# One input projection for two chunks: eight block products become seven, and the attention of those chunks is issued beside the third

## The chip, the cores and the metric

The kernel runs on one core of one Trainium2 chip. The metric is the device time of one execution, the median of the runs. Everything is float32. The engines are named as in the profile: PE (matmul), PEld (the loading of PE's weights), DVE (vector), ACT (scalar), POOL and SP, whose queue issues all DMAs here.

## The reference, cut to what matters

One encoder layer is applied to 1280 tokens: 1024 of a prompt and 256 of a sample, model width 1024.

```
h = x + 0.5 * swiglu(rmsnorm(x), gate, up, down)          # D_FF 2816
u = rmsnorm(h); proj = u @ w_in                           # 1024 -> 2816
aq, ak, av, rq, rk, rv, rg = split(proj)                  # 512,128,128,512,512,512,512
attn = rmsnorm(windowed attention with sink logits(rotate(aq), rotate(ak), av))
ret  = silu(rg) * norm(retention forward + retention backward(rotate(rq), rotate(rk), rv))
h = h + concat(attn, ret) @ w_out
h = h + 0.5 * swiglu(rmsnorm(h), gate2, up2, down2); y = rmsnorm(h)
```

The attention looks 128 tokens to both sides. Prompt and sample do not see each other.

## The kernel before, in words

**Layout.** Tokens lie along the free dimension, features along the 128 partitions. There are three chunks (`CH`, line 21): 0 and 1 are the two halves of the prompt, 512 tokens each, chunk 2 is the sample, 256 tokens. A "unit" is 128 output columns of a weight matrix with all 1024 rows; `w_in` has 22 units: four of `aq` (`UQ`), one each of `ak` (`UK`) and `av` (`UV`), four each of `rq`, `rk`, `rv` and of the gates `rg` (`URQ`, `URK`, `URV`, `URG`, line 23).

**Exactness.** Every operand of a large product is split into a high and a low fp32r half (`split`, line 510: one ACT copy, one DVE subtraction), and `part` (line 528) issues three matmuls for each 128 rows: high by high, high by low, low by high. One unit for one chunk is thus 8 x 3 = 24 matmuls.

**Stages.** The first feed-forward layer (`ffn`, line 655) already multiplies chunks 0 and 1 together by a seven-product scheme: `combos` (line 611) forms four sums of the activation blocks, `seven` (line 621) four sums of the weight blocks, and `product` (line 664) accumulates the seven products. `down_last` (line 793) ends the layer chunk by chunk. Then `project` (line 1044) computes each unit for each chunk: 22 units for chunk 0, 22 for chunk 1, 22 for chunk 2, and each time the unit's weights are fetched and split again. The result is rotated with tables (DVE), transposed on PE (the values), or put through Silu (the gates), and stays in SBUF; only the gates of chunk 0 go out to DRAM. The attention (`attention`, line 1081, eight blocks of 128 queries) and the retention (`retention`, line 1150, four heads) of chunks 0 and 1 are issued between the twelve head units of chunk 1; chunk 2's 22 projections come after them, with `cat_split(0)` (line 1239: norm and split of chunk 0's results) among them. `out_unit` (line 1249) is the product with `w_out`; then comes the second feed-forward layer.

**What sets the order.** `Weaver` (line 100) records all operations and plans their order: `arrange` (line 268) simulates the five engines with a cost for each operation (line 142) and takes, for each engine, the earliest operation of the program that is ready; operations of other engines than PE have priorities from the time at which PE needs them (`due`, line 254). The planned order of each engine is then fixed. An SP operation may be planned at most `AHEAD = 300` recorded operations before PE's front. Nearly all SBUF tiles are of one tag, `s2`: 104 buffers of 128x512 float32, and `may` (line 306) refuses an operation for which no buffer would be free. PSUM has eight banks under one tag. All calls go through line 438, so every row of the trace carries this line, and groups are told apart by the tiles' names: `pa` is a bank of the projections and feed-forward products, `pb` a bank of `down`, transposes and others, `pc` one of the scores; `wh` and `wl` are the halves of weights, `xh`, `xl` or `x` those of activations (`x` where W is 256).

Of the kernel before, what the change touches and what calls it, by code (L numbers as in the profile page):

```python
# [12 lines left out]
P = 128  # L13
# [86 lines left out]
class Weaver:  # L100
# [4 lines left out]
    MARGIN = 0.4  # L105
    AHEAD = 300
    PASSES = 4
    ENG = {"tensor": "PE", "vector": "DVE", "scalar": "ACT", "gpsimd": "POOL", "sync": "SP"}

    def __init__(self, tc):  # L110
# [157 lines left out]
    def arrange(self, prio):  # L268
# [37 lines left out]
        def may(op):  # L306
            if op.eng == "SP" and op.idx > front() + self.AHEAD:
                return False
            op.allocs = fresh(op)
            for b in op.allocs:  # L310
                t = self.tags[b.tag]
                need = sum(x.tag == b.tag for x in op.allocs)
                if len(t["free"]) < need:
                    return False
                gt = sorted(t["live"], reverse=True)
                j = 0
                m = b.order - 1
# [31 lines left out]
        table = None  # L349
        out = []  # L350
        SLACK = 0.15
        while len(out) < len(ops):
            best = None
            for e in engs:
                lim = free[e] + SLACK
                while later[e] and later[e][0][0] <= lim:
                    i = heapq.heappop(later[e])[1]
                    heapq.heappush(now[e], (prio[i], i))
                held = []
                pick = None  # L360
# [12 lines left out]
                if pick is None:  # L373
                    for r, i in sorted(later[e])[:40]:
                        if may(ops[i]):
                            pick = (r, i)
                            break
                if pick is not None:
                    op = ops[pick[1]]
                    start = pick[0]  # L380
                    for b in op.allocs:
                        start = max(start, min(self.tags[b.tag]["free"]))
                    if best is None or start < best[0]:
                        best = (start, pick[1], e)
            start, i, e = best
            op = ops[i]
            if (prio[i], i) in now[e]:
# [63 lines left out]
def tile_encoder_layer(ctx: ExitStack, tc: tile.TileContext, xT, wf1, w_in, w_out, wf2,  # L451
# [166 lines left out]
        nc.vector.scalar_tensor_tensor(t4, n2, -1.0, b21, op0=ALU.mult, op1=ALU.subtract)  # L618
        return {i: pair(t, 512) for i, t in ((6, n2), (7, t3), (5, t1), (4, t4))}

    def seven(r11, r12, r21, r22, W, together=False):

        if W > 256:
            s1, s2_, s3, s4 = (s2(name=n) for n in ("s1", "s2", "s3", "s4"))
# [12 lines left out]
        yield 21, halves(r21, W, together)  # L637
        nc.vector.tensor_tensor(s4, s2_, r12, op=ALU.add)
        yield 3, halves(s4, W, together)

# [275 lines left out]
    us = {}  # L916
    spill = {}

    def finish1(c):
        us[c] = norm_split(h[c], G_MIX, CH[c][1])  # L920

    def load1(c, d):
        return load_x(c, d, d + 1)[0]
# [63 lines left out]
    ffn(1, wf1, lead1(), lambda a: factors((a.n[0], a.n[1]), (a.pairs[0], a.pairs[1])), load1, after1, 1)  # L987


    mask = s2(name="mask")  # L990
    nc.sync.dma_start(mask[:, :384], cmat[:, 128:512])
    nc.sync.dma_start(cols, cmat[:, 512:520])
    sink8 = nc.tile(cpool, [P, 8], F32, None, "sink8", 1)
    nc.vector.tensor_scalar(sink8, par[:, SINK:SINK + 8], 8.0, None, op0=ALU.mult)
    dec = {}
    for name, ld, col in (("wf", LDF, 0), ("wb", LDB, 1), ("cf", LDF, 4), ("cb", LDB, 4)):
        t = nc.tile(cpool, [P, 4], F32, None, name, 1)
        nc.vector.tensor_scalar(t, par[:, ld:ld + 4], cols[:, col:col + 1], None, op0=ALU.mult)
        nc.scalar.activation(t, t, AF.Exp)
        if name[0] == "w":  # L1000
            nc.vector.tensor_scalar(t, t, KSC, None, op0=ALU.mult)
        dec[name] = t
    Dm = s2(name="Dm").rearrange("p (h i) -> p h i", h=4)
    rowf = s2(name="rowf").rearrange("p (h i) -> p h i", h=4)
    rowb = s2(name="rowb").rearrange("p (h i) -> p h i", h=4)
    ctm = s2(name="ctm")
    nc.sync.dma_start(ctm, cmat[:, 520:1032])
    ctr = s2(name="ctr")
    nc.sync.dma_start(ctr[:, 0:256], cmat[:, 1032:1288])
    for hh in range(4):  # L1010
        lf, lb = par[:, LDF + hh:LDF + hh + 1], par[:, LDB + hh:LDB + hh + 1]
        t1 = big(256, name="dt")
        nc.scalar.activation(t1[:, 0:128], ctm[:, 0:128], AF.Exp, scale=lf)
        nc.scalar.activation(t1[:, 128:256], ctm[:, 256:384], AF.Exp, scale=lb)
        nc.vector.tensor_tensor(t1[:, 0:128], t1[:, 0:128], ctm[:, 128:256], op=ALU.mult)
        nc.vector.tensor_tensor(t1[:, 128:256], t1[:, 128:256], ctm[:, 384:512], op=ALU.mult)
        nc.vector.tensor_tensor(t1[:, 0:128], t1[:, 0:128], t1[:, 128:256], op=ALU.add)
        nc.vector.tensor_scalar(Dm[:, hh, :], t1[:, 0:128], KSC, None, op0=ALU.mult)
        nc.scalar.activation(rowf[:, hh, :], ctr[:, 0:128], AF.Exp, scale=lf)
        nc.scalar.activation(rowb[:, hh, :], ctr[:, 128:256], AF.Exp, scale=lb)  # L1020


    o = {}

    pairs = {}
# [8 lines left out]
    def tables(c):  # L1034
        c0, W = CH[c]
        p0 = c0 if c < 2 else 0
        tabs = []
        for i in range(4):
            t = s2(name="tab")
            nc.sync.dma_start(t[:, :W], rope[:, i, p0:p0 + W])  # L1040
            tabs.append(t)
        return tabs

    def project(c, u, tabs):
        c0, W = CH[c]
        nb = W // P
        cosa, sina, cosr, sinr = tabs
        w = unit(w_in[u])
        ps = bank_a()
        lin(ps, w, us[c], W)  # L1050
        ps = ps[:, :W]
        out = new_out(c, u)[:, :W]
        o[c, u] = out
        if u >= URG:
            nc.scalar.activation(out, ps, AF.Silu)
            if c == 0:
                d = nc.tile(dp, [P, 512], F32, None, f"rg_{u}", 1)
                nc.sync.dma_start(d, out)
                o[c, u] = d
            return  # L1060
        t = big(W, name="rt")[:, :W]
        if u == UV or u >= URV:
            nc.scalar.copy(t, ps)
# [4 lines left out]
            return  # L1068
        if u <= UK:
            cos, sin = cosa, sina  # L1070
            nc.vector.stream_shuffle(t, ps, mask=SWAP)
        else:
            cos, sin = cosr, sinr
            nc.scalar.copy(t[0:64], ps[64:128])
            nc.scalar.copy(t[64:128], ps[0:64])
        nc.vector.tensor_tensor(out, ps, cos[:, :W], op=ALU.mult)
        nc.vector.tensor_tensor(t, t, sin[:, :W], op=ALU.mult)
        nc.vector.tensor_tensor(out, out, t, op=ALU.add)


    def attention(c, blk, chunks):
# [68 lines left out]
    def retention(hh, chunks):  # L1150
# [33 lines left out]
        for c in chunks:  # L1184
# [48 lines left out]
            if c == 0:  # L1233
# [26 lines left out]
            h[c][d] = t  # L1260


    lead = [UK, UV] + list(range(UQ, UQ + 4))
    heads = [b + hh for hh in range(4) for b in (URK, URV, URQ)]
    gates = list(range(URG, URG + 4))
    pr = (0, 1)
    tabs = tables(0)
    for i, u in enumerate(gates + [UV] + list(range(URV, URV + 4)) + [UK, 0, 1, 2, 3] + list(range(URQ, URV))):
        project(0, u, tabs)
        if i == 2:  # L1270
            finish1(1)
        if i == 5:
            finish1(2)
    tabs = tables(1)
    for u in gates + lead:
        project(1, u, tabs)
    todo = [(0, b) for b in range(4)] + [(1, b) for b in range(4)]
    for i, u in enumerate(heads):
        project(1, u, tabs)
        if i % 3 != 0:  # L1280
            attention(*todo.pop(0), pr)
        if i % 3 == 2:
            retention(i // 3, pr)
    tabs = tables(2)
    cat = {}
    for i, u in enumerate(gates + lead + heads):
        if i == 14:
            cat[0] = cat_split(0)
        project(2, u, tabs)
    for d in range(KT):  # L1290
        out_unit(0, d, cat[0])
        if d < 4:
# [131 lines left out]
```

## Time and profile before

| | |
|---|---|
| median of 3 runs | 2288.32 us (2284.65 to 2289.14) |
| the profiled execution, its own time | 2286.97 us |
| its span in the trace | 2285.0 us |
| PE busy | 2263.6 us, 99% of the span |
| PEld, DVE, ACT busy | 85%, 70%, 43% |
| granted PE clock, mean | 0.995 |
| DMA: bytes, mean rate | 330.63 MB, 145 GB/s |

Busy times of the engines overlap each other. PE counts as busy while any matmul is in flight, and matmuls are pipelined, so the spacing of starts tells more than the length of one. In a list of groups the mean of one instruction counts the part that overlaps the next; in a table of stretches the overlap is counted once. The projections and all that is woven into them lie between about 860 and 1295 us.

### The profile page before, as it was taken

How to read it: one execution, taken by the hardware profiler on the slowest of the kernel's cores; microseconds unless marked ns; L12 is line 12 of the kernel's file. 1: busy time of each engine (PE TensorE's matmuls, PEld its weight loads, DVE VectorE, ACT ScalarE, POOL GpSimd, SP SyncE). 2: the span in 40 equal slices, each digit the busy share in tenths (PEclk: the TensorE clock that was granted, in tenths of full speed). 3: DMA queues.
4: the chain of work that ended last, by engine and by line, in shares of the span. 5: the costliest groups of instructions: out<-in, count | busy, mean ns of one | idle time of the engine just before them, and what ended most of it. 6: DMA issues, size and time to landing. Idle time of an engine off the chain costs nothing.

```text
span 2285.0 us, 34157 instructions
## 1 busy us (share of the span) xinstructions
PE 2263.6 (99%) x12354; PEld 1936.0 (85%) x12354; DVE 1596.3 (70%) x3171; ACT 974.3 (43%) x2034; POOL 26.8 (1%) x31
## 2 busy tenths in 40 slices
PE   9999999999999999999999999999999999999998
PEld 8788888888888888887878978888888888888887
DVE  8966666556878876546779786676665566688856
ACT  7533443435412345234678373444443333432311
POOL 0000000000000000000000000000000000000000
PEclk9999999999999999999999999999999999999999
DMA  4333443345776634221125452244333334757722
GB/s 168 120 129 134 141 141 111 115 157 187 256 251 219 217 139 144 81 77 33 42 72 169 142 182 80 72 139 153 124 111 120 116 139 171 248 196 268 257 73 93
DMA packets 193417, 330.63 MB, mean 145 GB/s; under 512 B 20704, under 2 KB 45152, under 8 KB 193248
## 3 DMA queue, kind: packets, MB, share of 16 engines
q1 hardware_dynamic: 193248, 328.45, 42.0%
q8 instruction: 97, 1.59, 0.3%
q14 instruction: 72, 0.59, 0.1%
HBM read 226.65 MB, written 101.71 MB: 144 GB/s over the span
## 4 chain that ended last, share of the span: by engine, by line
PE 92%; DMA 4%; DVE 2%; issue 1%; ACT 1%; SPq 0%; POOL 0%; POOLq 0%; DVEq 0%; ACTq 0%
PE pa L438 64%; PE pb L438 27%; DMA raw<-wf 2%; PE pc L438 2%; DMA xa<-a 1%; DMA h<-xT 1%; ACT sq L438 0%; DMA raw<-w_in 0%; DVE xl L438 0%; DVE t L438 0%; DVE wl L438 0%; DVE s L438 0%; DMA h<-hf 0%; DMA a<-xh 0%; DMA a<-xl 0%
## 5 line engine op out<-in xcount | busy, mean ns | idle before, releaser
L438 PE MATMUL pa<-xh,wh 128*128 128x512 f32 x1664 | 656.6, 395 | 1.6 <-ACT xh L438 1.6
L438 PE MATMUL pa<-xl,wh 128*128 128x512 f32 x1664 | 650.4, 391 | 1.0 <-DVE xl L438 1.0
L438 PE MATMUL pa<-xh,wl 128*128 128x512 f32 x1664 | 649.0, 390 | 0.3 <-DVE wl L438 0.3
L438 PE MATMUL pb<-xa,w 128*128 128x512 f32 (+1 forms) x2376 | 452.8, 352 | 4.1 <-DVE h L438 3.1
L438 PEld LDWEIGHTS pb<-xa,w 128*128 128x128 f32 x2376 | 386.4, 189 | 70.6 <-DVE h L438 7.0
L438 PEld LDWEIGHTS pa<-xh,wl 128*128 128x128 f32 x1664 | 313.0, 188 | 67.2 <-DVE wl L438 0.7
L438 PEld LDWEIGHTS pa<-xh,wh 128*128 128x128 f32 x1664 | 313.6, 188 | 66.5 <-ACT xh L438 2.8
L438 PEld LDWEIGHTS pa<-xl,wh 128*128 128x128 f32 x1664 | 313.7, 189 | 60.0 <-DVE xl L438 1.8
L438 PE MATMUL pa<-x,wh 128*128 128x256 f32 x1824 | 337.0, 284 | 0.5 <-ACT wh L438 0.5
L438 PEld LDWEIGHTS pa<-x,wh 128*128 128x128 f32 x1824 | 293.0, 192 | 10.1 <-ACT wh L438 0.9
L438 DVE TENSOR_TENSOR wl<-raw,wh 128x512 fp32r<-128x512 f32 x372 | 243.8, 686 | 62.1 <-PE pa L438 27.8
L438 DVE SCALAR_TENSOR_TENSOR h<-pb,h 128x512 f32<-128x512 f32 (+1 forms) x360 | 223.7, 629 | 85.6 <-PE pb L438 81.8
L438 ACT CAST wh<-raw 128x512 fp32r<-128x512 f32 x372 | 215.7, 622 | 109.5 <-PE pa L438 47.4
L438 PE MATMUL pa<-x,wl 128*128 128x256 f32 x912 | 258.9, 284 | 0.5 <-DVE wl L438 0.4
L438 PEld LDWEIGHTS pa<-x,wl 128*128 128x128 f32 x912 | 175.1, 192 | 1.1 <-DVE wl L438 1.1
L438 ACT ACTIVATE o<-pa 128x512 f32<-128x512 f32 (+1 forms) x92 | 54.4, 591 | 239.6 <-PE pa L438 227.7
L438 DVE TENSOR_TENSOR o<-o,pa 128x512 f32<-128x512 f32 x120 | 81.9, 684 | 99.0 <-PE pa L438 98.4
L438 DVE TENSOR_TENSOR wl<-s,wh 128x512 fp32r<-128x512 f32 x160 | 107.0, 687 | 42.1 <-PE pa L438 29.7
L438 ACT CAST wh<-s 128x512 fp32r<-128x512 f32 x160 | 97.5, 619 | 58.2 <-PE pa L438 48.2
L438 ACT CAST w<-s 128x256 fp32r<-128x256 f32 x144 | 56.4, 406 | 134.4 <-DVE s L438 81.8
L438 DVE TENSOR_TENSOR s<-raw,raw 128x512 f32<-128x512 f32 (+1 forms) x116 | 70.1, 604 | 53.0 <-PE pa L438 42.8
L438 ACT ACTIVATE sq<-h 128x512 f32<-128x512 f32 (+1 forms) x96 | 51.1, 557 | 126.4 <-DVE h L438 124.6
(152 smaller groups left out, 2363.2 us busy)
## 6 DMA issues: line engine op xcount, KB each, us to landing
xa<-a SPq DMA_DIRECT2D x328, 256.0 KB, 5.1
raw<-wf SPq DMA_DIRECT2D x264, 256.0 KB, 4.5
a<-xh SPq DMA_DIRECT2D x142, 256.0 KB, 2.1
a<-xl SPq DMA_DIRECT2D x142, 256.0 KB, 3.4
raw<-w_in SPq DMA_DIRECT2D x132, 256.0 KB, 3.4
raw<-w_out SPq DMA_DIRECT2D x48, 256.0 KB, 3.6
a<-x SPq DMA_DIRECT2D x44, 256.0 KB, 2.1
h<-xT SPq DMA_DIRECT2D x32, 256.0 KB, 5.7
```

Source lines behind the costliest of these rows:

```text
L438: i = getattr(getattr(self.nc, eng), method)(*[r(x) for x in a], **{m: r(x) for m, x in k.items()})
```

## The change

The projections of chunks 0 and 1 are done together. `joint(u, v, xs)` takes two units and both chunks as a 2x2 block product and computes it with seven products of 4 x 3 matmuls (512 columns each) in place of eight; ten pairs of units go this way. The gate units `URG` and `URG+1` are still computed directly for both chunks, ahead of the pairs. The sums of the activations come from `factors` and `combos`, as in the feed-forward layers, so `finish1` now gives the normed activations and their halves for chunks 0 and 1, and chunk 2's norm stands behind the pairs. Every result of chunks 0 and 1 is shaped (`shape`, the former end of `project`) and then written to DRAM (`put`); before the attention and the retention the queries, keys and values are read back (`get`), and the gates of both chunks as before those of chunk 0. The eight attention blocks and four retention heads of chunks 0 and 1 are issued between the 22 projections of chunk 2. `cat_split(0)` stands behind all of these. The setup of masks and decays (formerly lines 990 to 1020) stands, unchanged, behind the pairs. The rotation tables are fetched at first use. In the planner a DMA may take an `s2` buffer only if six more than it needs are free (`LEAVE`); if nothing at all could be planned, this rule is lifted for one step.

```diff
+    LEAVE = 6
...
-                if len(t["free"]) < need:
+                if len(t["free"]) < need + (self.LEAVE if op.eng == "SP" and t["cap"] > 64 and not forced else 0):
                     return False
...
+            if best is None:
+                assert not forced
+                forced = True
+                continue
+            forced = False
...
     def finish1(c):
-        us[c] = norm_split(h[c], G_MIX, CH[c][1])
+        if c == 2:
+            us[c] = norm_split(h[c], G_MIX, CH[c][1])
+        else:
+            mx[c] = normed(h[c], G_MIX, 512)
+            mp[c] = [pair(t, 512) for t in mx[c]]
...
+    def put(c, u):
+        d = nc.tile(dp, [P, 512], F32, None, f"o_{c}_{u}", 1)
+        nc.sync.dma_start(d, o[c, u])
+        o[c, u] = d
+
+    def get(c, u):
+        t = s2(name="o")
+        nc.sync.dma_start(t, o[c, u])
+        o[c, u] = t
+
+    def joint(u, v, xs):
+        r = [fetch(w_in[a][:, i * 512:i * 512 + 512]) for a in (u, v) for i in range(2)]
+        X, Y, Z = bank_a(), bank_a(), bank_a()
+        for i, w in seven(*r, 512, alone=False):
+            if i == 1:
+                part(X, w, xs[1], 512, True, True)
+                o11 = s2(name="o11")
+                nc.scalar.copy(o11, X)
+            elif i == 2:
+                part(Z, w, xs[2], 512, True, True)
+                nc.vector.tensor_tensor(o11, o11, Z, op=ALU.add)
...
+            else:
+                part(X, w, xs[3], 512, False, True)
+        for c, a, x in ((0, u, o11), (0, v, o21), (1, v, o22), (1, u, X)):
+            shape(c, a, x, tabs[c], x is X)
+            put(c, a)
...
-    for i, u in enumerate(gates + [UV] + list(range(URV, URV + 4)) + [UK, 0, 1, 2, 3] + list(range(URQ, URV))):
-        project(0, u, tabs)
...
-    for u in gates + lead:
-        project(1, u, tabs)
-    todo = [(0, b) for b in range(4)] + [(1, b) for b in range(4)]
-    for i, u in enumerate(heads):
-        project(1, u, tabs)
-        if i % 3 != 0:
-            attention(*todo.pop(0), pr)
-        if i % 3 == 2:
-            retention(i // 3, pr)
...
-        if i == 14:
-            cat[0] = cat_split(0)
-        project(2, u, tabs)
+    for c in pr:
+        if c == 1:
+            finish1(1)
+        ps = [bank_a(), bank_a()]
+        for k in range(2):
+            for j in range(2):
+                part(ps[j], wg[j, k], mp[c][4 * k:4 * k + 4], 512, k == 0, k == 1)
+        for j in range(2):
+            shape(c, URG + j, ps[j], None, True)
+            put(c, URG + j)
+    xs = factors((mx[0], mx[1]), (mp[0], mp[1]))
+    joint(URG + 2, URG + 3, xs)
+    joint(UK, UV, xs)
+    joint(UQ, UQ + 1, xs)
+    joint(UQ + 2, UQ + 3, xs)
+    heads = [b + hh for hh in range(4) for b in (URK, URV, URQ)]
+    for i in range(6):
+        joint(heads[2 * i], heads[2 * i + 1], xs)
+    finish1(2)
...
+    for u in lead:
+        for c in pr:
+            get(c, u)
+    todo = [(c, b) for c in pr for b in range(4)]
+    for i in range(8):
+        if i % 2 == 0:
+            for b in (URK, URV, URQ):
+                for c in pr:
+                    get(c, b + i // 2)
+        attention(*todo[i], pr)
+        if i % 2 == 1:
+            retention(i // 2, pr)
+        for u in rest[i * 22 // 8:(i + 1) * 22 // 8]:
+            project(2, u, tabs[2])
+    cat[0] = cat_split(0)
```

## Rows read from the trace of the kernel before

**Rows 1.** The page's head: span, busy time and instructions of each engine.

```profile
span 2285.0 us, 34157 instructions
PE 2263.6 (99%) x12354; PEld 1936.0 (85%) x12354; DVE 1596.3 (70%) x3171; ACT 974.3 (43%) x2034; POOL 26.8 (1%) x31
```

**Rows 2.** Waits of PE from 780 to 1300 us: who for whom, us, times, longest.

```profile
PE pb L438 <- DVE h L438: 1.4, 1, 1.4
...
PE pb L438 <- ACT rt L438: 0.4, 1, 0.4
```

**Rows 3.** Chain that ended last, 780 to 1460 us: start, length, engine, bank, matmuls.

```profile
802.33 61.25 PE pb L438 x325
...
919.78 102.74 PE pa L438 x453
...
1246.04 17.28 PE pa L438 x144
```

**Rows 4.** Stretches: busy us of each engine (instructions), granted clock, DMA share, GB/s.

```profile
1045.00:1240.00 195.00, 194.53 (x1336) 155.93 (x1336) 153.44 (x467) 147.82 (x381) 8.35 (x8) 1.00 0.24 78
1200.00:1240.00 40.00, 39.95 (x322) 34.75 (x321) 37.09 (x105) 39.47 (x101) 2.30 (x2) 1.00 0.54 178
...
150.00:450.00 300.00, 300.00 (x1599) 259.82 (x1598) 194.63 (x323) 121.87 (x223) 0.00 (x0) 1.00 0.36 127
...
840.00:860.00 20.00, 20.00 (x122) 17.94 (x121) 19.35 (x36) 11.24 (x22) 0.00 (x0) 1.00 0.54 181
860.00:920.00 60.00, 60.00 (x301) 50.63 (x301) 37.19 (x71) 32.78 (x61) 1.70 (x2) 1.00 0.39 129
```

**Rows 5.** PE's groups from 1045 to 1240 us: projections; count, busy us, mean ns, idle before.

```profile
L438 PE MATMUL pa<-xh,wh 128*128 128x512 f32 x93 | 39.0, 419 | 0.0
L438 PE MATMUL pa<-xh,wl 128*128 128x512 f32 x94 | 36.8, 392 | 0.0
L438 PE MATMUL pa<-xl,wh 128*128 128x512 f32 x94 | 36.8, 391 | 0.0
...
L438 PE MATMUL pa<-x,wh 128*128 128x256 f32 x74 | 14.0, 289 | 0.0
...
L438 PE MATMUL pa<-x,wl 128*128 128x256 f32 x37 | 10.5, 283 | 0.0
```

**Rows 6.** DVE's and ACT's groups of the projections, 1045 to 1240 us.

```profile
L438 DVE TENSOR_TENSOR wl<-raw,wh 128x512 fp32r<-128x512 f32 x42 | 26.6, 684 | 0.0
...
L438 DVE TENSOR_TENSOR o<-o,rt 128x512 f32<-128x512 f32 x9 | 6.2, 689 | 0.2
L438 DVE TENSOR_TENSOR rt<-rt,tab 128x512 f32<-128x512 f32 x9 | 6.1, 681 | 0.0
...
L438 DVE TENSOR_TENSOR o<-pa,tab 128x512 f32<-128x512 f32 x8 | 5.5, 691 | 3.0 <-ACT rt L438 2.8
...
L438 ACT CAST wh<-raw 128x512 fp32r<-128x512 f32 x49 | 27.7, 636 | 0.0
...
L438 ACT COPY rt<-pa 64x512 f32<-64x512 f32 (+1 forms) x20 | 11.6, 582 | 55.6 <-PE pa L438 55.4
```

**Rows 7.** Groups of the whole span: a product's sum, and chunk 2's rotation (1235 to 1300).

```profile
L438 DVE TENSOR_TENSOR o<-o,pa 128x512 f32<-128x512 f32 x120 | 81.9, 684 | 99.0 <-PE pa L438 98.4
...
L438 DVE TENSOR_TENSOR o<-o,rt 128x256 f32<-128x256 f32 x13 | 5.5, 425 | 0.4
```

**Rows 8.** DVE's instructions in order of time, 838 to 862 us: start, length, count.

```profile
846.85 2.48 DVE L438 SCALAR_TENSOR_TENSOR h<-pb,h 128x512 f32<-128x512 f32 x4
849.25 0.68 DVE L438 TENSOR_TENSOR sq<-sq,sq 128x512 f32<-128x512 f32 x1
```

**Rows 9.** DMA issues: count, KB each, median us from issue to landing.

```profile
hs<-h SPq DMA_DIRECT2D x16, 256.0 KB, 2.1
...
rg<-rg SPq DMA_DIRECT2D x4, 256.0 KB, 2.5
```

More of the change, by code (lines that the diff above doesn't have):

```diff
@@ L384, in arrange @@
                         best = (start, pick[1], e)
+            if best is None:
+                assert not forced
+                forced = True
+                continue
+            forced = False
             start, i, e = best
@@ L619, in combos, with seven @@
         return {i: pair(t, 512) for i, t in ((6, n2), (7, t3), (5, t1), (4, t4))}
-    def seven(r11, r12, r21, r22, W, together=False):
+    def seven(r11, r12, r21, r22, W, together=False, alone=True):
         if W > 256:
@@ L636, in seven @@
         yield 4, halves(r22, W, together)
-        yield 21, halves(r21, W, together)
+        if alone:
+            yield 21, halves(r21, W, together)
         nc.vector.tensor_tensor(s4, s2_, r12, op=ALU.add)
@@ L917, in tile_encoder_layer @@
     spill = {}
+    mx, mp = {}, {}
     def finish1(c):
[L920 removed]
+        if c == 2:
[3 more added lines that the diff above has]
+            mp[c] = [pair(t, 512) for t in mx[c]]
     def load1(c, d):
@@ L987, in tile_encoder_layer @@
     ffn(1, wf1, lead1(), lambda a: factors((a.n[0], a.n[1]), (a.pairs[0], a.pairs[1])), load1, after1, 1)
[L990 to L1020, printed above, removed]
     o = {}
@@ L1036, in tables, with tab, shape @@
         p0 = c0 if c < 2 else 0
[L1037 to L1042, printed above, removed]
+        tabs = {}
+        def tab(i):
+            if i not in tabs:
+                tabs[i] = s2(name="tab")
+                nc.sync.dma_start(tabs[i][:, :W], rope[:, i, p0:p0 + W])
+            return tabs[i]
+        return tab
     def project(c, u, tabs):
-        c0, W = CH[c]
-        nb = W // P
-        cosa, sina, cosr, sinr = tabs
         w = unit(w_in[u])
         ps = bank_a()
-        lin(ps, w, us[c], W)
-        ps = ps[:, :W]
+        lin(ps, w, us[c], CH[c][1])
+        shape(c, u, ps, tabs, True)
+    def shape(c, u, src, tabs, banked):
+        W = CH[c][1]
+        nb = W // P
+        src = src[:, :W]
         out = new_out(c, u)[:, :W]
@@ L1054, in project @@
         if u >= URG:
[L1055 to L1059, printed above, removed]
+            nc.scalar.activation(out, src, AF.Silu)
             return
-        t = big(W, name="rt")[:, :W]
         if u == UV or u >= URV:
-            nc.scalar.copy(t, ps)
+            t = src
+            if banked:
+                t = big(W, name="rt")[:, :W]
+                nc.scalar.copy(t, src)
             pt = bank_b()
@@ L1068, in project @@
             return
+        t = big(W, name="rt")[:, :W]
         if u <= UK:
-            cos, sin = cosa, sina
-            nc.vector.stream_shuffle(t, ps, mask=SWAP)
-        else:
[L1073 to L1076, printed above, removed]
+            cos, sin = tabs(0), tabs(1)
+            nc.vector.stream_shuffle(t, src, mask=SWAP)
+        else:
+            cos, sin = tabs(2), tabs(3)
+            nc.scalar.copy(t[0:64], src[64:128])
+            nc.scalar.copy(t[64:128], src[0:64])
@@ L1077, in project @@
+        nc.vector.tensor_tensor(out, src, cos[:, :W], op=ALU.mult)
         nc.vector.tensor_tensor(t, t, sin[:, :W], op=ALU.mult)
         nc.vector.tensor_tensor(out, out, t, op=ALU.add)
+    def put(c, u):
[17 more added lines that the diff above has]
+                nc.vector.tensor_tensor(o11, o11, Z, op=ALU.add)
+            elif i == 6:
+                part(X, w, xs[6], 512, False, True)
+                o21 = s2(name="o21")
+                nc.scalar.activation(o21, X, AF.Copy, scale=-1.0)
+            elif i == 7:
+                part(Y, w, xs[7], 512, True, True)
+                o22 = s2(name="o22")
+                nc.scalar.activation(o22, Y, AF.Copy, scale=-1.0)
+            elif i == 5:
+                part(X, w, xs[5], 512, False, True)
+                nc.vector.tensor_tensor(o22, o22, X, op=ALU.subtract)
+            elif i == 4:
+                part(Y, w, xs[4], 512, False, True)
+                nc.vector.tensor_tensor(o21, o21, Y, op=ALU.subtract)
+            else:
[3 more added lines that the diff above has]
+            put(c, a)
@@ L1232, in retention @@
             g = o[c, URG + hh]
-            if c == 0:
+            if c < 2:
                 g = s2(name="rg")
@@ L1260, in out_unit @@
             h[c][d] = t
-    lead = [UK, UV] + list(range(UQ, UQ + 4))
[L1264 to L1267, printed above, removed]
-    for i, u in enumerate(gates + [UV] + list(range(URV, URV + 4)) + [UK, 0, 1, 2, 3] + list(range(URQ, URV))):
-        project(0, u, tabs)
[L1270 to L1274, printed above, removed]
-    for u in gates + lead:
-        project(1, u, tabs)
@@ L1277, in tile_encoder_layer @@
-    todo = [(0, b) for b in range(4)] + [(1, b) for b in range(4)]
-    for i, u in enumerate(heads):
-        project(1, u, tabs)
-        if i % 3 != 0:
-            attention(*todo.pop(0), pr)
-        if i % 3 == 2:
-            retention(i // 3, pr)
-    tabs = tables(2)
-    cat = {}
-    for i, u in enumerate(gates + lead + heads):
-        if i == 14:
-            cat[0] = cat_split(0)
-        project(2, u, tabs)
+    pr = (0, 1)
+    tabs = {c: tables(c) for c in range(3)}
+    wg = {(j, k): halves(fetch(w_in[URG + j][:, k * 512:(k + 1) * 512])) for j in range(2) for k in range(2)}
@@ new lines, in tile_encoder_layer @@
+    heads = [b + hh for hh in range(4) for b in (URK, URV, URQ)]
+    for i in range(6):
+        joint(heads[2 * i], heads[2 * i + 1], xs)
+    finish1(2)
+    mask = s2(name="mask")
+    nc.sync.dma_start(mask[:, :384], cmat[:, 128:512])
+    nc.sync.dma_start(cols, cmat[:, 512:520])
+    sink8 = nc.tile(cpool, [P, 8], F32, None, "sink8", 1)
+    nc.vector.tensor_scalar(sink8, par[:, SINK:SINK + 8], 8.0, None, op0=ALU.mult)
+    dec = {}
+    for name, ld, col in (("wf", LDF, 0), ("wb", LDB, 1), ("cf", LDF, 4), ("cb", LDB, 4)):
+        t = nc.tile(cpool, [P, 4], F32, None, name, 1)
+        nc.vector.tensor_scalar(t, par[:, ld:ld + 4], cols[:, col:col + 1], None, op0=ALU.mult)
+        nc.scalar.activation(t, t, AF.Exp)
+        if name[0] == "w":
+            nc.vector.tensor_scalar(t, t, KSC, None, op0=ALU.mult)
+        dec[name] = t
@@ new lines, in tile_encoder_layer @@
+    Dm = s2(name="Dm").rearrange("p (h i) -> p h i", h=4)
+    rowf = s2(name="rowf").rearrange("p (h i) -> p h i", h=4)
+    rowb = s2(name="rowb").rearrange("p (h i) -> p h i", h=4)
+    ctm = s2(name="ctm")
+    nc.sync.dma_start(ctm, cmat[:, 520:1032])
+    ctr = s2(name="ctr")
+    nc.sync.dma_start(ctr[:, 0:256], cmat[:, 1032:1288])
+    for hh in range(4):
+        lf, lb = par[:, LDF + hh:LDF + hh + 1], par[:, LDB + hh:LDB + hh + 1]
+        t1 = big(256, name="dt")
+        nc.scalar.activation(t1[:, 0:128], ctm[:, 0:128], AF.Exp, scale=lf)
+        nc.scalar.activation(t1[:, 128:256], ctm[:, 256:384], AF.Exp, scale=lb)
+        nc.vector.tensor_tensor(t1[:, 0:128], t1[:, 0:128], ctm[:, 128:256], op=ALU.mult)
+        nc.vector.tensor_tensor(t1[:, 128:256], t1[:, 128:256], ctm[:, 384:512], op=ALU.mult)
+        nc.vector.tensor_tensor(t1[:, 0:128], t1[:, 0:128], t1[:, 128:256], op=ALU.add)
+        nc.vector.tensor_scalar(Dm[:, hh, :], t1[:, 0:128], KSC, None, op0=ALU.mult)
+        nc.scalar.activation(rowf[:, hh, :], ctr[:, 0:128], AF.Exp, scale=lf)
+        nc.scalar.activation(rowb[:, hh, :], ctr[:, 128:256], AF.Exp, scale=lb)
@@ new lines, in tile_encoder_layer @@
+    lead = [UK, UV] + list(range(UQ, UQ + 4))
+    rest = list(range(URG, URG + 4)) + lead + heads
+    for u in lead:
+        for c in pr:
+            get(c, u)
+    todo = [(c, b) for c in pr for b in range(4)]
+    cat = {}
+    for i in range(8):
[8 more added lines that the diff above has]
+            project(2, u, tabs[2])
```

## The prediction

> **What bounds the kernel now.** The page's head first: PE is busy in 2263.6 of 2285.0 us, DVE in 70% and ACT in 43% [rows 1]. That share alone proves little, since a pipelined engine looks busy with gaps in it; so the next views are PE's waits and the chain. From 780 to 1300 us, the stretch that the change rewrites, PE waited for others 2.2 us in all, in three waits, of which the longest and the shortest are shown [rows 2]. On the chain the same stretch is PE almost throughout: one piece is 453 matmuls of 512 columns in 102.74 us, that is 0.2268 us each [rows 3]; another is 144 matmuls of 256 columns in 17.28 us, 0.120 us each [rows 3]. The clock was granted in full there [rows 4]. So PE issues without a gap, and time goes away only with PE's work, as long as nobody else becomes late. The reader is to see both things: the steps of PE, and how full its suppliers are in each stretch.
>
> [...] I go by the spacing of starts.
>
> **The change part by part.**
>
> *Removed from PE.* A pair of units for two chunks was 4 x 24 = 96 matmuls and becomes 7 x 4 x 3 = 84. Ten pairs: 120 matmuls of 512 columns, at 0.2268 us [rows 3] 27.2 us. Gates `URG` and `URG+1`, chunk 2's 528 matmuls, the transposes, attention, retention and all that follows keep their count. Nothing is added to PE. **-27.2 us**, if PE stays without gaps.
>
> *The start.* The gates and the first two products need only norms; the products 6, 7, 5 and 4 need the sums of the activations: 16 DVE sums and 16 DVE subtractions for the halves. Four subtractions in a row start 0.60 us apart (846.85 to 849.25) though each lasts 0.68 [rows 8], so this is 19.2 us; the norm of chunk 1, now needed at once, has 16 such (9.6 us), the gates' weights 4 (2.4 us), the first pair's weights 11 (6.6 us): 37.8 us of DVE from the moment chunk 1's `h` is complete, about 853, and DVE is already 97% full before that (19.35 of 20) [rows 4]. PE has in hand: the end of the first layer until 863.6 [rows 3], 96 gate matmuls (21.8 us) and two products (5.4 us), so until 890.8: 38 us. The two are equal, the last sums are needed up to 11 us later, and PE can run the first two products of the next pair (5.4 us) in between. Bounds 0 and 8 us (the late sums with no cover); the cover is there, so near the low end: **+2**.
>
> *The ten pairs.* For one pair DVE has 7 subtractions, 4 weight sums and 3 sums of results, 14 x 0.60 = 8.4 us; the rotations of a unit and chunk are 3 more, 4 for the attention's. The two pairs of queries are the worst: 8.4 + 16 x 0.60 = 18.0 us beside 84 x 0.2268 = 19.1 of PE. Over all ten: 140 + 88 operations, 137 us beside 190 of PE, 72%. A stage of the same make, the products of the first layer, runs DVE at 65% with PE at 100% [rows 4]; a sum of a result out of its bank is 684 ns there [rows 7], like the others. Its idle DVE says that this scheme alone costs PE nothing. The weights' DMAs fall from 132 to 88; writes and reads of results grow by 40 each. Such a transfer takes 2.1 and 2.5 us to land [rows 9], and the DMA engines are 24% to 54% busy in the attention's stretch [rows 4]. What is new is the queue: a `put` waits on SP until DVE has shaped its tile, and behind it stand the next pair's weight fetches, for which ACT's splits and then PE wait. Covered while fetches are planned more than 3 us ahead; if not, some 1 us per pair. Bounds 0 and 10, **+1**.
>
> *Chunk 2 with attention and retention.* This is the step that decides. Before, attention and retention of the first chunks lay in 1045 to 1240. PE there: 194.5 us, less 281 matmuls of 512 columns (63.7) and 111 of 256 (13.3) [rows 4, 5]: 117.5 us. Chunk 2 adds 528 x 0.120 = 63.4: PE has 181 us in the new stretch. DVE there: 153.4 us, less the projections' groups, 26.6 + 6.2 + 6.1 + 5.5 [rows 4, 6]: 109. Chunk 2 adds 44 subtractions of 684 ns (30.1), 39 rotations of 425 ns (16.6) [rows 6, 7], and chunk 0's norm and split, some 15 of 0.68 (10): 166 us, 92% of 181; with the new ones at their distance of 0.60 to 0.68, 159 us, 88%. ACT: 147.8 - 27.7 - 11.6 + 44 x 0.636 + about 12 for chunk 2's copies and the split = 149, 82% [rows 4, 6]. Before, this work had DVE at 79% over 195 us. So the stretch goes from comfortable to tight, and both suppliers are in a chain through PE (scores, maximum, exponent, transposes, values). For it speaks the stretch 1200 to 1240: DVE 93% and ACT 99% busy, and PE still 39.95 of 40 [rows 4]; the planner had found an order without gaps at that density. A gain is excluded, since PE had no gaps to lose. Bounds 0 and 29 us (DVE no fuller than before, worked out under the rivals). I take a value near the row at 93%: **+4**.
>
> [...]
>
> *The end of that stretch.* `cat_split(0)` had eight of chunk 2's projections behind it (23 us); now its last input, head 3's retention, comes with three projections behind it (8.6 us). PE has seven eighths of the first output unit (4.8 us) and chunk 2's retention besides. Bounds 0 and 6, **+1**.
>
> *The planner's new rule.* `LEAVE` holds for both feed-forward layers too, where it makes fetches start when six more buffers are free, and every plan comes out somewhat other than before. Weights there are fetched four at a time for some 20 us of matmuls, so a delay is covered. Bounds -3 and +8 (0.2 us at each of about 40 block changes), **0**.
>
> *Sum,* against the profiled execution: 2286.97 - 27.2 + 2 + 1 + 4 + 1 = 2267.8. The median of the runs is 1.35 us above that execution (2288.32), so 2269.1: **2269 us**.
>
> **The rivals.**
>
> *DVE becomes the bound beside chunk 2 (slower).* If attention and retention cannot keep DVE fuller than the 79% they reached before (153.4 of 195), because each step waits for PE or ACT in turn, 166 us of work take 166 / 0.79 = 210 us in place of 181: +29, the whole saving. Time 2269 - 4 + 29 = 2294. It decides from 166 / (181 + 27) = 80% on: below that share the kernel is slower. For it: DVE had 21% idle there, mostly waiting for PE and ACT, and the 22 projections that followed as free filler are now spent inside. Against it: the 93% and 99% from 1200 to 1240 [rows 4], and PE, not DVE, set the pace of the old stretch.
>
> *DVE and the queue hold up the start and the pairs.* Both terms at their upper bounds, 8 + 10 in place of 3: 2284. For it: equal supply and need at the start, 95% in the queries' pairs, 56 of 104 buffers held by activations. Against it: the first layer's stage at 300.00 of 300.
>
> *The rule of six buffers starves the feed-forward layers.* +8: 2277. For it: they are three quarters of the time. Against it: their DVE and DMA have slack [rows 4].
>
> *The removed products are not seen at all,* PE spending the time in waits at other places: 2287. The rows speak against it as above.
>
> **How the numbers follow.** A measurement of this kernel tells 0.2%, 4.6 us, from no change: 2283.7 to 2292.9 is the same. My forecast has 0.62, its own range 2260 to 2277. DVE beside chunk 2: 0.15, of which 0.12 slower and 0.03 the same. Start and pairs: 0.12, half faster, half the same. The six buffers: 0.09, faster. Not seen: 0.02, the same. Faster 0.62 + 0.06 + 0.09 = 0.77; same 0.03 + 0.06 + 0.02 = 0.11; slower 0.12. The range takes in all but the slow end (some 0.15) and a little below: 2259 to 2288.
>
> **What would show it.** PE's matmul instructions fall by about 120, and the pairs stand at 0.227 us a step. In the stretch with chunk 2, PE 181 us long or a few more, DVE near 88% to 92%, ACT above 80%, PE's waits for probabilities, `pt` or `wl` a few us in sum. At the start, PE waits for `xl` or `xh` of the sums, under 3 us. In the feed-forward layers nothing. I am wrong if PE's waits from 860 us to `w_out` sum to over 15 us, if DVE's share beside chunk 2 stays near 80%, or if the layers' lengths move by more than 3 us.

## The result and the profile after

The changed kernel takes **2271.85 us** (median; 2270.64 to 2273.01), the kernel before 2287.63 in the same runs: ratio **0.9934, 95% interval 0.9922 to 0.9947**, some 15 us faster. The forecast was 2269 us, so the saving was put about 4 us too high. A second set of runs of the same kernel gave 0.9938 (0.9924 to 0.9951).

The page's head after, for [rows 1]:

```profile
span 2268.7 us, 34074 instructions
PE 2236.5 (99%) x12234; PEld 1916.9 (84%) x12234; DVE 1646.5 (73%) x3259; ACT 982.7 (43%) x2058; POOL 27.7 (1%) x31
```

PE had 12354 matmul instructions and has 12234: the 120 are gone. The spans differ by 16.3 us. To see where, lay the two traces over each other at groups that both have. Here are, of the kernel before and then of the changed one, the last down stage of the first layer (`xa,wh`, in the first 1000 us) and chunk 0's and 1's output units (`ch,wh`); the two times are the first and the last start.

```profile
L438 PE MATMUL pb<-xa,wh x192: 278/389/486, 806.3 to 863.2; 128*128 128x512 f32 x128, 128*128 128x256 f32 x64
...
L438 PE MATMUL pa<-ch,wh x64: 389/389/496, 1296.2 to 1406.8; 128*128 128x512 f32 x64
```

```profile
L445 PE MATMUL pb<-xa,wh x192: 277/389/486, 804.2 to 860.8; 128*128 128x512 f32 x128, 128*128 128x256 f32 x64
...
L445 PE MATMUL pa<-ch,wh x64: 389/389/504, 1279.0 to 1387.8; 128*128 128x512 f32 x64
```

The last down stage of the second layer starts at 2214.7 before and 2198.7 after. That gives four pieces:

| piece | before | after | difference |
|---|---|---|---|
| start to the first layer's last down stage | 806.3 | 804.2 | -2.1 |
| from there to `ch,wh`, the stretch that was rewritten | 489.9 | 474.8 | **-15.1** |
| from there to the second layer's last down stage | 918.5 | 919.7 | +1.2 |
| rest | 70.3 | 70.0 | -0.3 |

So the rewritten stretch gave 15.1 us where 27.2 us of matmuls are gone: **12.1 us were lost in it**. Here is that stretch as one row, before and after, in columns as in [rows 4]; the busy time of PE comes first behind the length:

```profile
806.30:1296.20 489.90, 489.07 (x2920) 411.06 (x2919) 342.30 (x811) 261.74 (x591) 12.07 (x12) 1.00 0.30 98
```

```profile
804.20:1279.00 474.80, 466.67 (x2821) 396.01 (x2821) 396.93 (x920) 284.69 (x641) 13.16 (x12) 0.99 0.38 126
```

PE was idle for 0.8 us of it and is now idle for 8.1 us, and the mean granted clock is no longer 1.00. The idle time stands in PE's waits (for [rows 2]; from 780 to 1440 us, those above 0.4 us; the third lies behind the stretch):

```profile
PE pb L445 <- DVE xn L445: 4.4, 1, 4.4
PE pb L445 <- issue: 3.5, 1, 3.5
PE pa L445 <- DVE h L445: 0.5, 1, 0.5
```

The clock fell around the first two of them. Stretches after: first the gates and pairs, then the stretch beside chunk 2, then small steps around the two waits:

```profile
861.00:1084.50 223.50, 223.50 (x1026) 184.49 (x1025) 182.84 (x325) 106.33 (x196) 1.94 (x2) 1.00 0.36 120
1084.50:1262.00 177.50, 173.78 (x1417) 151.31 (x1417) 156.28 (x495) 144.65 (x382) 7.63 (x7) 0.99 0.38 125
1084.00:1086.00 2.00, 0.53 (x4) 0.29 (x4) 2.00 (x6) 1.64 (x5) 0.00 (x0) 1.00 0.83 302
1086.00:1088.00 2.00, 0.00 (x0) 0.00 (x0) 2.00 (x7) 2.00 (x6) 0.00 (x0) 0.84 0.85 280
1088.00:1090.00 2.00, 1.96 (x10) 1.98 (x11) 1.97 (x9) 2.00 (x9) 0.00 (x0) 0.50 1.03 368
1090.00:1092.00 2.00, 2.00 (x15) 2.00 (x15) 1.90 (x11) 1.95 (x7) 0.00 (x0) 0.80 1.06 386
1270.00:1272.00 2.00, 0.00 (x0) 0.00 (x0) 2.00 (x4) 2.00 (x5) 0.00 (x0) 0.92 0.05 18
1272.00:1274.00 2.00, 0.31 (x1) 0.18 (x1) 2.00 (x5) 0.61 (x2) 0.00 (x0) 0.50 0.81 276
1274.00:1276.00 2.00, 2.00 (x6) 1.58 (x6) 1.97 (x5) 0.19 (x1) 0.00 (x0) 0.50 0.86 291
1276.00:1278.00 2.00, 2.00 (x6) 1.60 (x5) 1.97 (x4) 0.00 (x0) 0.00 (x0) 0.50 0.62 220
1278.00:1280.00 2.00, 2.00 (x9) 1.58 (x8) 1.80 (x3) 0.00 (x0) 0.00 (x0) 0.87 0.00 0
```

Read the PE column against the clock, the third figure from the end. Over the gates and all ten pairs PE is busy 223.50 us of 223.50, at a clock of 1.00. At 1084.5, the hand-over to the attention, it is idle 3.5 us, and when it resumes the clock stands at 0.50 for about 3 us: 0.5 x 1.96 + 0.2 x 2 = 1.4 us of work lost. At 1269 it is idle 4.4 us and then has 0.50 until about 1278.5: 1.0 + 1.0 + 0.5 x 0.31 + 0.13 x 2 = 2.4 us lost. The two waits, 7.9 us, and 3.8 us lost at half clock are 11.7 of the 12.1 us. The account is good to a microsecond or two and no better: the kernel before had 0.8 us of idle time there too, and 21 small matmuls (about 2.3 us at some 0.11 us each) lie ahead of the first `ch,wh` in the changed kernel that came behind it before. In steps of 0.25 us, from 1086 to 1092, 1271 to 1273 and 1278 to 1279.25, the clock is 1.00 or 0.50 except in the four steps in which it changes (0.74, 0.94, 0.88, 0.97); the 0.80 to 0.92 of the rows above are stretches that hold both.

What each wait is, the order of time shows. PE and DVE around the second one (start, length, what, idle time before it and its end):

```profile
1268.88 0.39 PE L445 MATMUL pc<-o,o 128*128 128x128 f32 x2
1273.69 0.45 PE L445 MATMUL pb<-ident,o 128*128 128x128 f32 x1 [4.42 <-DVE xn L445]
1274.08 0.77 PE L445 MATMUL pa<-xh,wh 128*128 128x512 f32 x1
1274.64 0.63 PE L445 MATMUL pa<-xl,wh 128*128 128x512 f32 x1
1275.07 0.63 PE L445 MATMUL pa<-xh,wl 128*128 128x512 f32 x1
```

```profile
1268.42 0.68 DVE L445 TENSOR_TENSOR cl<-o,ch 128x512 fp32r<-128x512 f32 x1
1269.02 2.06 DVE L445 SCALAR_TENSOR_TENSOR xn<-o,par,pb 128x512 f32<-128x512 f32 x3
1270.99 1.89 DVE L445 TENSOR_TENSOR xl<-xn,xh 128x512 fp32r<-128x512 f32 x3
1272.80 0.74 DVE L445 SCALAR_TENSOR_TENSOR xn<-o,par,pb 128x512 f32<-128x512 f32 x1
```

Chunk 0's attention norm (`xn`) runs only from 1269.0 on, and PE started the last matmul of chunk 2's projections at 1264.5; the output unit needs the norm: that is `cat_split(0)` at the end. PE's queue is further headed by a transpose into a `pb` bank that the last `xn` releases, though the first `xl` came earlier; a bank that the norm still reads would explain it, which was not tried. The matmuls of 512 columns then start 0.43 us apart, against 0.227. In the first wait the waiting instruction is again a transpose, of keys read back from DRAM, while DVE and ACT are full (2.00 of 2.00 us from 1086 to 1088), mostly with chunk 2's norm, without which PE has no projection of chunk 2 to run; DMA stands at 0.83 to 1.06 in the rows above. Two causes offer themselves there, the late norm and the late read-back.

### The profile page after: what moved, and what is told of

Read it like the earlier page. It is cut to its first block, busy times and chain, and to the rows that moved or that the text cites. A ratio compares the mean times of both kernels' runs of the same rounds, so it can differ in the third digit from the quotient of the medians.

```text
span 2268.7 us, 34074 instructions
## 1 busy us (share of the span) xinstructions
PE 2236.5 (99%) x12234; PEld 1916.9 (84%) x12234; DVE 1646.5 (73%) x3259; ACT 982.7 (43%) x2058; POOL 27.7 (1%) x31
## 4 chain that ended last, share of the span: by engine, by line
PE 89%; DMA 5%; DVE 3%; ACT 1%; issue 1%; SPq 0%; POOL 0%; POOLq 0%; DVEq 0%; ACTq 0%
PE pa L445 62%; PE pb L445 25%; DMA raw<-wf 2%; PE pc L445 1%; DMA xa<-a 1%; DMA h<-xT 1%; DVE h L445 1%; DVE xl L445 1%; DMA h<-hf 0%; DVE s L445 0%; ACT sq L445 0%; DVE wl L445 0%; SPq L445 0%; DVE w L445 0%; DVE t L445 0%
## 5 line engine op out<-in xcount | busy, mean ns | idle before, releaser
L445 PE MATMUL pa<-xh,wh 128*128 128x512 f32 x1624 | 637.3, 392 | 3.2 <-ACT xh L445 2.7
L445 PE MATMUL pa<-xl,wh 128*128 128x512 f32 x1624 | 634.4, 391 | 1.3 <-DVE xl L445 1.3
L445 PE MATMUL pa<-xh,wl 128*128 128x512 f32 x1624 | 632.8, 390 | 0.0
L445 DVE TENSOR_TENSOR wl<-raw,wh 128x512 fp32r<-128x512 f32 x318 | 211.0, 687 | 33.8 <-PE pa L445 15.2
L445 ACT CAST wh<-raw 128x512 fp32r<-128x512 f32 x318 | 186.4, 621 | 95.8 <-DMA raw<-w_in 43.0
L445 DVE TENSOR_TENSOR o<-o,pa 128x512 f32<-128x512 f32 x150 | 102.3, 684 | 137.9 <-PE pa L445 125.9
L445 DVE TENSOR_TENSOR wl<-s,wh 128x512 fp32r<-128x512 f32 x200 | 134.1, 688 | 30.9 <-PE pa L445 20.8
L445 ACT CAST wh<-s 128x512 fp32r<-128x512 f32 x200 | 118.6, 619 | 47.5 <-PE pa L445 24.5
L445 ACT CAST w<-raw 128x256 fp32r<-128x256 f32 x144 | 53.2, 404 | 147.0 <-DMA raw<-wf 95.0
L445 DVE TENSOR_TENSOR xl<-s,xh 128x512 fp32r<-128x512 f32 x70 | 48.4, 692 | 88.1 <-ACT xh L445 85.7
```

The source lines that it names most:

```text
L445: i = getattr(getattr(self.nc, eng), method)(*[r(x) for x in a], **{m: r(x) for m, x in k.items()})
```

## The experiments

Ratios are to the kernel before, with 95% intervals. "Stretch" is the time from the first `xa,wh` to the first `ch,wh` in the profiled execution: 474.8 us in the changed kernel, 475.9 in its second set of runs.

**1. Chunk 2's norm earlier.**

```diff
-    finish1(2)
...
         joint(heads[2 * i], heads[2 * i + 1], xs)
+        if i == 3:
+            finish1(2)
```

> Chunk 2's norm (finish1(2)) is issued after the fourth of the six head pairs instead of behind all ten pairs; else the changed kernel. Theory A: PE's 3.5 us wait at the hand-over from the pairs to the attention (1084.5 us), with the half clock after it, came because chunk 2's projections, the only work free of the attention's chain, lacked their norm; then the wait and the dip of the clock go, about 1.3 + 3.5 us: 2267 us. Rival B: the wait is for the keys read back from DRAM, and filler makes no difference to what is late: wait stays over 3 us, 2272. Rival C: the eight buffers that the norm holds longer slow the last pairs: 2273 to 2276.

Measured: 2270.98 us, 0.9932 (0.9918 to 0.9945). The wait and its dip are gone: the clock is 1.00 from 1080 to 1100, so the place of the norm, not the read-back, decides whether PE stops there. PE fills the time with chunk 2's projections, from 1086.0 on; DVE is also rid of the norm at that moment, and the run does not tell the two apart. But the stretch is 475.2 us. The attention's first masked score comes 4.5 us later on DVE (1084.9 for 1080.4), small waits for `pt`, `rt`, `r` and `mx` appear, and the 4.4 us at the end stand: PE's waits from 850 to 1340 us sum to 8.2 us, against 8.4 in the changed kernel. The local cause was right; the gain was not kept.

**2. Chunk 0's norm earlier.**

```diff
+        if i == 4:
+            cat[0] = norm_split([o[0, UQ + g] for g in range(4)], G_ATT, 512)
...
-    cat[0] = cat_split(0)
+    for u in range(URQ, URQ + 4):
+        a, b = two(512, "c")
+        split(o[0, u], a, b)
+        cat[0][0].append(a)
+        cat[0][1].append(b)
```

> The norm of chunk 0's attention output is issued after its fourth attention block (before block 5 of 8) instead of behind all of chunk 2's projections; only the splits of the retention outputs stay at the end. Theory A: PE's 4.4 us wait for that norm at 1269 us and the half clock until 1278 us (2.1 us of work lost) go: 2265 us. Rival B: DVE is full there (2.00 of 2.00 us in each stretch from 1270 to 1274), so the wait only turns into one for another DVE result: 2269 to 2272, with PE idle over 3 us between 1240 and 1300.

Measured: 2267.45 us, 0.9917 (0.9904 to 0.9931), stretch 471.1. PE's waits from 850 to 1340 us:

```profile
PE pb L445 <- issue: 3.5, 1, 3.5
PE pa L445 <- DVE xn L445: 2.8, 1, 2.8
PE pc L445 <- DVE xn L445: 0.9, 1, 0.9
```

The wait at the end is gone, from 1240 to 1300 PE is busy 59.98 of 60 us and the clock is 1.00. The same norm now holds PE up in the middle, at 1181 us, 3.7 us in two pieces, with a dip to 0.91 over 20 us. Gain 3.7 us of the 6.8: each theory had a part.

**3. The eighth product put back.**

```diff
-        for i, w in seven(*r, 512, alone=False):
+        for i, w in seven(*r, 512):
...
+            elif i == 21:
+                part(bank_a(), w, xs[2], 512, True, True)
```

> Each of the ten pairs also computes an eighth product of 12 matmuls (weights r21 by the second activation block) into a bank that nobody reads, so PE has the matmul count of the kernel before while everything else of the change stays. Theory A: the pairs go at PE's pace, 120 x 0.2268 = 27 us come back: 2299 us, about 11 us above the kernel before, which is what the hand-over and the end cost. Rival B: the pairs are paced by DVE or by the result traffic, PE has room: under 2285 us.

Measured: 2304.19 us, 1.0076 (1.0063 to 1.0088). The stretch is 503.2 us, 28.4 longer than the changed kernel's, against 27.2 worked out; from 863 to 1110 us, gates and pairs, PE is busy all the time:

```profile
863.00:1110.00 247.00, 247.00 (x1126) 205.47 (x1126) 188.25 (x326) 109.39 (x201) 1.01 (x1) 1.00 0.32 107
```

The pairs go at PE's pace, and the 120 products are worth what the spacing says. The edit also adds ten weight splits on ACT and DVE. The whole kernel is 32 us slower than the changed one; 4.6 us of that lie ahead of the stretch in the profiled execution (808.8 for 804.2), where no operation was edited. With the eighth products, the rest of the change costs 13 us in this stretch over the kernel before (503.2 - 489.9).

**4. The planner's rule alone, in the kernel before.**

```diff
+    LEAVE = 6
...
+                if len(t["free"]) < need + (self.LEAVE if op.eng == "SP" and t["cap"] > 64 and not forced else 0):
...
```

> The kernel before with the planner's new rule alone (a DMA takes a large buffer only if six more are free). Theory A: the rule makes no difference of its own, the feed-forward layers' small gains and losses (first layer 2.3 us shorter, second 2.8 us longer in the changed kernel) are other orders and other dips of the clock: 2286 to 2291 us. Rival B: the rule starves the layers: 2294 to 2296. Rival C: the rule is itself worth the first layer's gain and costs the second's: first layer again near 574 us to its down stage, second near 230.5 us in its down stage.

Measured: 2287.11 us, 1.0005 (0.9996 to 1.0014): nothing in the time. But the trace has both shifts that rival C named. The first layer's down stage begins at 574.0 us (577.1 before, 574.2 in the changed kernel), and the second layer's takes 230.4 us from the first `xa,w` to the first `xa,wh` (227.4 before, 230.5 in the changed kernel). They cancel, and they are not the rule's alone: experiments 1 and 2 have the rule too, and their second layer's down stage takes 227.9 and 227.4 us.

**5. Both norms earlier** (chunk 2's at `i == 1`, chunk 0's at `i == 6`, edits as in 1 and 2).

> Both moves at once: chunk 2's norm is issued after the second of the six head pairs, the norm of chunk 0's attention output after the sixth attention block. Theory A: the two waits are separate costs, the hand-over's wait and the end's wait with their dips go together: some 2265 us or, with the first experiment's return of the same loss in small waits, 2266. Rival B: the stretch beside chunk 2 is held by DVE and ACT, and what is won at the two places comes back inside it: 2269 to 2272.

Measured: **2262.79 us, 0.9898 (0.9884 to 0.9912)**, faster than both kernels. The stretch is 465.8 us, 9.0 shorter than the changed kernel's:

```profile
805.60:1271.40 465.80, 462.67 (x2801) 390.85 (x2800) 391.90 (x910) 284.42 (x639) 12.59 (x12) 1.00 0.38 126
```

Of the 9.0 us, 5.0 are idle time of PE (3.1 for 8.1) and 3.8 the half clock; the small matmuls stand behind the marker again, so this split too is good to a microsecond or two, and up to the last `ch,wh` the gain is 7.4 us (576.2 for 583.6). PE's waits from 850 to 1340 us are five small ones:

```profile
PE pa L445 <- DVE o L445: 1.2, 2, 0.7
PE pb L445 <- ACT prob L445: 0.7, 2, 0.4
PE pb L445 <- ACT rt L445: 0.7, 1, 0.7
PE pb L445 <- ACT pt L445: 0.4, 1, 0.4
PE pc L445 <- ACT pt L445: 0.3, 1, 0.3
```

with the clock at 1.00 throughout (stretches of the projections, the attention and the end):

```profile
862.40:1271.40 409.00, 405.87 (x2498) 341.63 (x2497) 350.69 (x841) 261.17 (x599) 11.58 (x11) 1.00 0.37 122
1084.00:1262.00 178.00, 175.68 (x1423) 150.25 (x1424) 158.87 (x493) 145.80 (x382) 7.94 (x8) 1.00 0.39 127
1260.00:1280.00 20.00, 20.00 (x133) 18.21 (x133) 17.59 (x51) 9.35 (x22) 2.32 (x3) 1.00 0.71 223
```

DVE does the same work in the whole kernel (1648.6 us, 1646.5 in the changed one), and its share of the stretch is 84% in both (391.90 of 465.80, 396.93 of 474.80): the shorter stretch needed no fuller DVE.

**6. Less work for DVE beside chunk 2.** Its queries and keys are left unrotated.

```diff
+        if c == 2:
+            if u > UK:
+                t = big(W, name="rt")[:, :W]
+                nc.scalar.copy(t[0:64], src[64:128])
+                nc.scalar.copy(t[64:128], src[0:64])
+            nc.vector.tensor_copy(out, src)
+            return
```

> Chunk 2's queries and keys are left unrotated: one DVE copy of 256 columns in place of three or four DVE operations in 13 units, some 11 us of DVE less in the stretch beside chunk 2; PE's and ACT's work stays. The output of the sample is not the reference's. Theory A: PE's waits there are chains (norm, read-back) and not DVE's load: the wait at the end stays near 4 us, the time falls by 0 to 3 us: 2269 to 2272. Rival B: DVE's load (88% to 100%) is the bound: the waits shrink and the time falls by 6 us or more: 2266 or below.

Measured: 2271.38 us, 0.9937 (0.9924 to 0.9949). DVE's work falls by 9.8 us in all (1636.7 for 1646.5), by 8.2 from 1084.5 to 1262 (148.11, 83% of it, for 156.28, 88%), and the time does not move: waits of 3.5 us at the hand-over and 3.5 at the end remain. The mean clock here is 0.83 from 1080 to 1100, 0.87 from 1260 to 1280 and 0.96 from 1280 to 1300; in the changed kernel it is 0.91, 0.83 and 1.00, in its second set 0.91, 0.86 and 0.97. Over the 60 us, idle time counted, 6.8 us of clock are missing here and 5.2 in each of the two sets, so a gain of a microsecond or two could be hidden; one of 6 us, as the rival asked, could not. That is the plainest evidence against the rival.

**7. The gap filled with matmuls that nobody reads.**

```diff
     cat[0] = cat_split(0)
+    idle = bank_a()
+    for _ in range(32):
+        nc.tensor.matmul(idle[:, 0:256], lhsT=us[2][0][0][:, 0:128], rhs=us[2][0][0][:, 0:256], start=True, stop=True)
```

> 32 matmuls of 256 columns that nobody reads (3.8 us) stand between chunk 2's projections and the first output unit, where PE waits 4.4 us for chunk 0's norm. Theory A: the half clock after that wait comes from the idle time alone, so with the gap filled the granted clock stays at 1.00 from 1270 to 1280 and the 2.1 us lost there come back, although no useful work is added: 2270 us, the first output unit's matmuls 0.227 us apart from the start. Rival B: the clock falls anyway, or the filler delays the output units: 2272 to 2276.

Measured: 2269.32 us, 0.9924 (0.9910 to 0.9937), which the runs can't tell from the changed kernel; the profiled execution is the fastest of its five. The trace shows the gap:

```profile
1270.00:1272.00 2.00, 2.00 (x16) 1.82 (x15) 2.00 (x4) 1.99 (x5) 0.00 (x0) 1.00 0.19 50
1272.00:1274.00 2.00, 2.00 (x11) 1.67 (x10) 1.97 (x4) 1.11 (x2) 0.00 (x0) 1.00 0.96 302
1274.00:1276.00 2.00, 2.00 (x10) 1.65 (x9) 1.99 (x5) 0.00 (x0) 0.00 (x0) 1.00 0.52 172
1276.00:1278.00 2.00, 2.00 (x11) 1.65 (x10) 1.94 (x3) 0.00 (x0) 0.00 (x0) 1.00 0.74 239
```

The clock stays at 1.00, two microseconds hold 10 or 11 matmuls instead of 6, and from `xa,wh` to the last `ch,wh` it is 581.4 us instead of 583.6. The half clock came from the idle time. Part of the 2.2 us can be chance, since the second set of the changed kernel has 584.9.

**8. The changed kernel without the planner's rule** (`LEAVE = 0`).

> The changed kernel without the planner's new rule (LEAVE = 0). Theory A: the rule has no cost or gain beyond other orders, within 3 us of the changed kernel: 2269 to 2275. Rival B: the rule keeps buffers free for the results read back and is worth over 4 us beside chunk 2: 2276 or above, with new PE waits from 1080 to 1280 us.

Measured: 2274.48 us, 0.9952 (0.9940 to 0.9965). The stretch is as it was (474.9); the first layer reaches its last down stage 2.8 us later (807.0), and PE's waits up to 850 us sum to 13.4 us there, 10.3 in the changed kernel. The time is in theory A's range and the intervals overlap, so a worth of the rule for the whole is not shown.

**9. The changed kernel again.**

> The changed kernel once more, on the chip of the next two. Every theory: ratio to the kernel before 0.993, about 2270 to 2273 us; it gives the level against which the next two are read.

Measured: 2271.95 us, 0.9938 (0.9924 to 0.9951). The same program, and yet not the same clock: from 100 to 120 us 0.91 here and 1.00 in the first profile, with a first layer 0.9 us longer (805.1 to 804.2).

**10. Chunk 2's norm alone, behind the second head pair.**

> Chunk 2's norm alone moved, to behind the second head pair, as in the combined version. Theory A: what the first experiment won at the hand-over (3.5 us and a dip of the clock) came back as small waits because the attention's chain, not PE's filler, sets when the stretch ends; then here too the first output unit starts within 1.5 us of the changed kernel's (474.8 us after the last down stage) and the time is that of the changed kernel. Rival B: the place after the fourth pair was bad for the last pairs, and at this place the gain is kept: first output unit 4 to 5 us earlier, some 4 us shorter than the changed kernel.

Measured: 2270.09 us, 0.9934 (0.9922 to 0.9947), stretch 472.4, 2.4 to 3.5 us shorter, wait at the end unchanged, though the mean clock from 1260 to 1280 is 0.91 in place of 0.83 and 0.86. In the stretch it lies between the two theories; in the time it is theory A, since from `ch,wh` to the second layer's last down stage it takes 922.8 us, 2.7 to 3.1 more than the changed kernel (919.7 and 920.1), where nothing was edited; a wait for `h` in the second layer is 3.4 us there, 2.6 and 2.0 in the changed kernel's two sets.

**11. The combined version without the planner's rule.**

> Both moves of the combined version, with the planner's new rule off. Theory A: the rule only changes orders: within 3 us of the combined version, ratio to the kernel before about 0.990 to 0.992. Rival B: without it the first layer is slower, as in the eighth experiment (2.8 us to the last down stage): ratio 0.992 or more, with the down stage at 577 us.

Measured: 2269.15 us, 0.9936 (0.9924 to 0.9949); its interval does not meet that of 5. The first layer reaches its last down stage at 809.9 (805.6 in 5) and the stretch is 470.2 (465.8). Here the rule, or the order that comes with it, is worth 6 us by the medians and 9 by the ratios; PE's waits up to 850 us sum to 15.2 us without it and 11.0 with it. In the kernel before it was worth nothing.

## Why the prediction was right, and where it was not

- **Removed from PE, -27.2:** right; 120 instructions, and experiment 3 gives them back at 28.4 us in the stretch.
- **The start, +2, and the pairs, +1:** both 0. PE was busy 223.50 of 223.50 us. DVE was at 82% there, in the middle of what was worked out (72% for the pairs alone, full at the start).
- **Beside chunk 2, +4:** about right, for another reason. The sum of loads was good: 88% for DVE (156.28 of 177.50) and 81% for ACT (144.65), against 88% to 92% and 82%. But the 3.5 us of waiting and 1.4 us at half clock that were lost came at one place, the hand-over, where chunk 2's norm, moved behind the pairs, left PE without filler. The description of the change names that move, and the prediction gave it no price: that +4 and 4.9 are close is luck. On DVE's spacing: the four operations 0.60 us apart in [rows 8] are sums of `h`, not subtractions; in the profile after, the three subtractions `xl` from 1270.99 to 1272.80 start 0.60 us apart too.
- **The end, +1:** this is the step that failed. `cat_split(0)` behind all projections cost 4.4 us, and 2.4 more at half clock: 6.8 us, above the upper bound of 6. The cover that was counted, three projections and chunk 2's retention, was used up before: the planner gives PE the earliest ready work, so it had started the last projection's last matmul at 1264.5 and the last of the retention that was ready at 1268.9, before the norm began at 1269.0. And "seven eighths of the first output unit" were no cover, since a unit's products go in order into one bank and begin with the attention's norm.
- **The clock:** no term of the sum had it, and it cost 3.8 us.
- **The planner's rule, 0:** the first layer moved by -2.1, the second layer's down stage by +3.1, just over the 3 us that were to be a sign of being wrong; from `ch,wh` on the piece moved by +1.2. The rule alone has the same two shifts (experiment 4). Dips of the clock at the start differ between two executions of the changed kernel (1.00 and 0.91 from 100 to 120 us, experiment 9), so not all of this is the kernel's.
- **The sum:** the misses partly cancel, 3 us too much for the start and the pairs, some 6 too little for the end, 1 too little beside chunk 2. That the total came within 4 us is in part luck.
- **The rivals:** "DVE becomes the bound" is refuted by 88% busy, where it needed DVE to stay near 79%, and by experiments 5 and 6. The second rival did not occur. Nor did the third: with the rule off the kernels are not faster (8, 11), and the rule alone costs the kernel before nothing (4). The last is refuted by experiment 3.

What stays open: why an earlier norm of chunk 2 alone (1, 10) keeps little or half of what it wins, while with the other move (5) the stretch gains 9.0 us, more than 3.7 and 2.4 together. In 5 chunk 0's norm stands at `i == 6`, in 2 at `i == 4`, where it made a new wait of 3.7 us; `i == 6` alone was not run, so the place and the interaction are not told apart. The moves can also interact through the planned order; the attention's later first score in experiment 1 is what was seen, not a shown cause.

## What to carry to other kernels

Where PE has no gaps, count the matmuls removed, at the spacing of their starts, and then ask of each piece of filler work what it waits for and when it is spent: two norms that were moved to the end of their stages took some 12 of 27 us, and other places for them gave some 9 back. Price a wait of some 4 us on PE at more than its length: here the matmuls behind it ran at half clock and lost 1.4 to 2.4 us more. And before taking a full engine for the bound, take some of its work away: here some 10 us less changed nothing.

## What the runs showed of the hardware

In the profile shown the granted clock fell while PE was still idle (0.84 from 1086 to 1088, 0.92 from 1270 to 1272); in steps of 0.25 us it went from 1.00 to 0.50 some 2.8 us into the first wait (at about 1087.4) and 2.4 us into the second (at about 1271.7). After the idle 3.5 us PE ran some 3 us at 0.50, after the idle 4.4 us some 5 us; matmuls of 256 columns stepped at 0.21 us behind the first wait, those of 512 at 0.43 behind the second. The price varies: with the same 4.4 us the mean clock from 1260 to 1280 was 0.83 in the changed kernel, 0.86 in its second set (and 0.97 in the 20 us after) and 0.91 in experiment 10. The waits of up to 0.7 us in experiment 5 left the clock at 1.00. Filling the gap with idle products kept 1.00, with 10 or 11 matmuls in two microseconds for 6 (experiment 7), and such products, in a gap that was there anyway, gave 2.2 us back in this trace; the times of the runs do not show it.
